# Modulation vectors on VectorE, spread over two layers, and other matmul figures in a planner's cost table

## The chip, the cores and the metric

The kernel runs on one core of a Trainium2 chip, as one launch. The metric is the device time of that launch in microseconds. Every time below is from three timed runs of the kernel before, or from one further execution that was recorded by the hardware profiler.

## What is computed

Two models stand behind each other, on 512 tokens of width 1024 in float32. The first has two hybrid layers: a gated delta rule (GDN, four heads), latent attention (MLA, eight heads) and a linear recurrence (LRU), each behind one input projection, then an output projection that is added to x. The second model has one layer with differential attention, a two-way retention and a mixture of 64 experts. It needs six modulation vectors, which depend on no token:

```python
mod_x = silu(c) @ ada_w + ada_b           # c: (1, 1024), ada_w: (1024, 6144)
mod_c = silu(c_ctx) @ ada_w + ada_b
sh1, sc1, g1, sh2, sc2, g2 = split(mod_x, 6)     # of mod_c the layer uses sh1 and sc1
hx = rmsnorm(x) * (1 + sc1) + sh1                # first use, once both hybrid layers are done
```

So the work on the modulation (called ada in the code) can be done at any time before the second model begins, in the shadow of the two hybrid layers.

## The kernel before

The kernel does not call the engines directly. Every operation is first recorded (class Rec, method add) with its inputs, its outputs and a duration from a table of costs (Rec.cost), in nanoseconds. Then a list scheduler (Rec.plan and Rec.attempt) sets the order of each engine's instructions and of the DMA queue on SyncE: of the operations that are ready by its own clock, the one with the highest priority (the longest remaining path, plus a bias) goes next, if the buffers that it needs are free. The order is then fixed in the program; on the chip each engine runs its own list in that order and waits where an input is late. All instructions are issued from one helper line, so line numbers tell nothing in this profile, and groups are told apart by tile names: raw are seven buffers of 128x1024 for weights that come by DMA, b are 128x512 work buffers, m small ones, ps the eight PSUM banks.

A hybrid layer goes like this. Its input is normalized and transposed (norm_T), and weights of the input projection are loaded in blocks of 512 KB (raw<-in_wi_dram). Each block is split on ScalarE and VectorE into a rounded high part and a low rest (split: an ACTIVATE and a TENSOR_TENSOR for each 128x512), and three fp32r matmuls stand for one product (mm3). TensorE thus waits for VectorE's splits, and VectorE also empties PSUM. In a first stage the chain of GDN is merged with the dense projections; in a second one the eight attention heads are merged with output projections. K.layer merges generators by weights, and a third generator, side, may be merged into both stages: that is ada. The layer ends with x written to DRAM for a later use (xd<-b), by layer 0 and by layer 1 alike.

K2.ada takes the six parts of ada_w in blocks of 128x1024, eight for each part: 48 loads of 512 KB (raw<-in_adaw_dram) into four of the raw buffers (tag ad). Parts 0 and 1 are needed for two vectors, so there are 64 products of a block with a column of numbers: ScalarE scales the block, and GpSimd adds it to the accumulator, but for the first product of each accumulator, which stands alone (64 ScalarE instructions, 56 GpSimd ones). A matmul with a vector of ones then sums over the partitions. K2.ahead wraps that generator: it raises the bias of its operations by 1,000,000, so that whichever is ready goes before anything else on its engine. With the weights SIDE, the generator ends within layer 0. Two lists of windows (WIN, WINA) hold other operations back by their place in the recording.

## Time and profile before

| | us |
|---|---|
| median of three runs | 2389.94 (2387.89 to 2395.32) |
| profiled execution | 2396.73 |
| its span, first to last instruction | 2395.0 |
| TensorE busy | 2187.3 (91%) |
| VectorE busy | 1619.6 (68%) |
| ScalarE busy | 1087.7 (45%) |
| GpSimd busy | 534.6 (22%) |

The profiled execution is 6.79 us above the median, and lies 1.73 us above its own span. Busy time on TensorE is modelled and counts pipelined matmuls whole. In a row of a timeline the first number is the start in us from the span's start, the second the duration; x3 merges three instructions that follow each other; brackets give the idle time before and what ended it. A chain of waits follows the work that ended last back through what released it.

### The profile page before, as it was taken

What the parts mean: (1) busy time and instruction counts of PE and PEld (TensorE: products, weight loads), DVE (VectorE), ACT (ScalarE), POOL (GpSimd) and SP (SyncE); (2) the same over time, 40 slices, a digit from 0 to 9 for tenths busy, and PEclk for the clock granted to TensorE, in tenths of its full rate; (3) what the DMA queues carried; (4) which work ended last, traced back from release to release, by engine and by line L of the source; (5) the groups of instructions that cost most, each with busy time, mean ns of one, the idle gap of its engine ahead of it and who ended that gap; (6) DMA issues with size and microseconds to landing.
All of it is one profiled execution on the core that took longest, in us unless ns stands there. A gap on an engine that the chain in (4) does not pass through costs nothing.

```text
span 2395.0 us, 32613 instructions
## 1 busy us (share of the span) xinstructions
PE 2187.3 (91%) x10382; PEld 1546.5 (65%) x10382; DVE 1619.6 (68%) x3578; ACT 1087.7 (45%) x2272; POOL 534.6 (22%) x393
## 2 busy tenths in 40 slices
PE   6898988999999999999998879879998999999995
PEld 4677866677788877777886657656555555444442
DVE  7995577775695557767733675657676667776775
ACT  5555456453452365445432353335444444544443
POOL 3364334200021010001000132033232233222222
PEclk9998999899999999999998979989999999999998
DMA  5334354223222232314211025349999899999994
GB/s 191 119 102 127 118 172 146 86 84 124 94 78 74 78 116 75 92 63 143 71 54 53 23 66 198 132 116 348 288 341 282 267 294 313 340 334 302 307 311 130
DMA packets 191185, 398.13 MB, mean 166 GB/s; under 512 B 32169, under 2 KB 48297, under 8 KB 191010
## 3 DMA queue, kind: packets, MB, share of 16 engines
q1 hardware_dynamic: 178050, 356.24, 44.1%
q0 software_dynamic: 12960, 39.79, 7.6%
q8 instruction: 82, 1.34, 0.2%
q14 instruction: 93, 0.76, 0.1%
HBM read 358.44 MB, written 41.63 MB: 167 GB/s over the span
## 4 chain that ended last, share of the span: by engine, by line
PE 69%; DVE 13%; DMA 11%; ACT 3%; issue 3%; POOL 1%; SPq 0%; POOLq 0%; DVEq 0%; ACTq 0%
PE ps L411 69%; DVE b L411 10%; DMA raw<-h2d,m 5%; DVE m L411 3%; ACT b L411 3%; DMA accd<-raw,m 1%; DMA raw<-in_adaw_dram 1%; DMA raw<-in_wo_dram 1%; DMA b<-in_ew_dram 1%; POOL raw L411 1%; DMA xdiag<-b 0%; DMA raw<-in_wi_dram 0%; SPq L411 0%; DMA raw<-accd 0%; DMA b<-in_x_dram 0%
## 5 line engine op out<-in xcount | busy, mean ns | idle before, releaser
L411 PE MATMUL ps<-b,b 128*128 128x512 f32 (+9 forms) x8052 | 1870.1, 389 | 83.2 <-DVE b L411 49.6
L411 PEld LDWEIGHTS ps<-b,b 128*128 128x128 f32 (+6 forms) x8052 | 1312.6, 184 | 571.9 <-issue 130.1
L411 ACT ACTIVATE b<-ps 128x512 f32<-128x512 f32 (+16 forms) x661 | 271.1, 431 | 676.6 <-PE ps L411 599.6
L411 DVE TENSOR_TENSOR b<-b,b 128x512 fp32r<-128x512 f32 (+5 forms) x751 | 469.8, 664 | 35.2 <-ACT b L411 18.3
L411 ACT ACTIVATE b<-b 128x512 fp32r<-128x512 f32 (+3 forms) x702 | 393.8, 619 | 121.6 <-DVE b L411 84.5
L411 DVE TENSOR_TENSOR b<-raw,b 128x512 fp32r<-128x512 f32 (+2 forms) x340 | 240.0, 720 | 187.2 <-ACT b L411 173.7
L411 ACT ACTIVATE b<-raw 128x512 fp32r<-128x512 f32 (+3 forms) x348 | 207.2, 611 | 350.3 <-PE ps L411 256.0
L411 POOL DMA_INDIRECT accd<-raw,m x72 | 133.2, 1850 | 367.6 <-DVE raw L411 224.3
L411 PE MATMUL ps<-const,b 128*128 128x128 f32 (+5 forms) x898 | 159.5, 292 | 52.1 <-DVE b L411 39.0
L411 PEld LDWEIGHTS ps<-const,b 128*128 128x128 f32 (+5 forms) x898 | 115.0, 153 | 102.0 <-DVE b L411 49.4
L411 POOL TENSOR_TENSOR raw<-raw,raw 128x1024 f32<-128x1024 f32 x56 | 140.2, 2512 | 159.9 <-ACT raw L411 132.3
L411 PE MATMUL ps<-raw,b 128*96 128x512 f32 (+5 forms) x272 | 151.8, 676 | 5.3 <-ACT raw L411 2.9
L411 POOL DMA_INDIRECT raw<-h2d,m x68 | 100.9, 1483 | 231.0 <-PE ps L411 83.7
L411 DVE SCALAR_TENSOR_TENSOR raw<-ps,m,b 96x512 f32<-96x512 f32 (+5 forms) x136 | 97.5, 740 | 50.9 <-DMA accd<-raw,m 30.1
L411 DVE SCALAR_TENSOR_TENSOR b<-b,ps 128x512 f32<-128x512 f32 (+6 forms) x106 | 54.1, 510 | 102.7 <-ACT b L411 99.2
L411 POOL TENSOR_TENSOR m<-m,mhalf 128x1 f32<-128x1 f32 (+2 forms) x54 | 52.2, 968 | 301.6 <-DVE m L411 301.6
L411 DVE TENSOR_REDUCE m<-ps 128x1 f32<-128x256 f32 (+9 forms) x196 | 75.1, 393 | 60.5 <-PE ps L411 59.0
L411 DVE TENSOR_TENSOR b<-b,ps 128x512 f32<-128x512 f32 (+6 forms) x150 | 82.6, 559 | 49.2 <-PE ps L411 48.5
L411 DVE TENSOR_TENSOR b<-ps,b 128x512 fp32r<-128x512 f32 (+8 forms) x136 | 74.0, 545 | 47.1 <-ACT b L411 38.9
L411 POOL MEMSET b<- 64x512 f32 (+4 forms) x19 | 8.4, 454 | 398.1 <-PE ps L411 326.6
L411 DVE SCALAR_TENSOR_TENSOR b<-ps,cols,b 128x511 f32<-128x511 f32 (+3 forms) x118 | 86.9, 742 | 7.8 <-ACT b L411 6.9
L411 PE MATMUL ps<-const,raw 96*128 96x96 f32 (+5 forms) x544 | 61.0, 249 | 33.4 <-DMA raw<-h2d,m 30.4
(139 smaller groups left out, 1199.0 us busy)
## 6 DMA issues: line engine op xcount, KB each, us to landing
b<-in_ew_dram SPq DMA_DIRECT2D x640, 256.0 KB
raw<-in_wi_dram SPq DMA_DIRECT2D x100, 512.0 KB
raw<-in_ew_dram SPq DMA_DIRECT2D x64, 512.0 KB
raw<-in_adaw_dram SPq DMA_DIRECT2D x48, 512.0 KB
raw<-in_wo_dram SPq DMA_DIRECT2D x40, 512.0 KB
raw<-in_wuq_dram SPq DMA_DIRECT2D x24, 192.0 KB
b<-in_x_dram SPq DMA_DIRECT2D x16, 256.0 KB
zd<-b SPq DMA_DIRECT2D x16, 256.0 KB
```

The costliest lines, as they stand in the source:

```text
L411: getattr(getattr(nc, o.eng), o.fn)(*[real(x) for x in o.a], **{m: real(x) for m, x in o.k.items()})
```

## The change

GpSimd's part in ada goes. Where ScalarE scaled a block and GpSimd added it, VectorE now does both in one instruction (scalar_tensor_tensor, 128x1024, with the column of numbers as its scalar and the accumulator as in place input and output). The first product of each accumulator stays on ScalarE. So 56 ScalarE and 56 GpSimd instructions are replaced by 56 VectorE ones.

The generator is cut into portions of 14 steps: 14 in each of the two stages of layer 0, then in those of layer 1 (there are 54 steps, nine for each part). And each of its operations gets a gate: it cannot be planned before the operation that was recorded 60 earlier has been.

In the table of costs an fp32r matmul with at least 256 columns costs 0.4167 ns a column plus 14 ns, where it was plus 3; a float32 one costs 24 ns more, with a floor of 224 where it was 216. These numbers change no instruction, but the order of all of them.

```diff
--- before.py
+++ after.py
@@ -2,6 +2,7 @@
 import heapq
 import math
 from contextlib import ExitStack
+from itertools import islice
 
 import numpy as np
 
@@ -33,13 +34,15 @@
 XAHEAD = 6
 XBIAS = 6900.0
 NATIVE = 4
-SIDE = ((160, 351), (130, 122))
+SIDE = (11, 12.5)
+SIDEN = 14
 NSLOT = 80
 NADA = 4
 TAGS = {"wl": 5, "wh": 5, "s2": None}
 NRAW = 7
 ADAPS = "tr"
 ADABIAS = 1000000.0
+ADALEAD = 60
 TAIL = 200
 WIDE = (4, 6)
 LAST = 1
@@ -311,8 +314,8 @@
             if dt == BF16:
                 return max(w, 54)
             if dt == F32R:
-                return w + 3 if size(ins[1]) >= 256 else max(4 * w, 108)
-            return max(4 * w, 216)
+                return w + 14 if size(ins[1]) >= 256 else max(4 * w, 108)
+            return max(4 * w + 24, 224)
         if eng == "scalar":
             return 70 + 0.87 * n + (200 if len(outs) > 1 else 50 if len(ins) > 1 else 0)
         if eng == "vector":
@@ -1373,7 +1376,7 @@
         self.pairs, self.mixB = {}, []
         dense = chain(self.lru(l), self.mla_lat(l), self.mz(l))
         parts = [(self.gdn_chain(l), GW[l]), (dense, 100)]
-        run(merge(*parts, *([(side, SIDE[l][0])] if side else [])))
+        run(merge(*parts, *([(islice(side, SIDEN), SIDE[0])] if side else [])))
         self.load_x()
         self.rope_tables(self.A["const"], 256)
         src = lambda nh, k: self.A["wo"][l, nh, k]
@@ -1388,7 +1391,7 @@
                 if h == 3:
                     self.part = list(self.mixB)
 
-        run(merge((heads(), 100), (dense, 60), *([(side, SIDE[l][1])] if side else [])))
+        run(merge((heads(), 100), (dense, 60), *([(islice(side, SIDEN), SIDE[1])] if side else [])))
         run(self.out_proj(src, 4, self.part))
         run(self.out_proj(src, 8, self.mixB[4:8], last=True))
         self.dump_x(f"x{l}")
@@ -1433,12 +1436,14 @@
         g = iter(g)
         while True:
             self.nc.bias += ADABIAS
+            self.nc.gate = max(len(self.nc.ops) - ADALEAD, 0)
             try:
                 w = next(g)
             except StopIteration:
                 return
             finally:
                 self.nc.bias -= ADABIAS
+                self.nc.gate = None
             yield w
 
     def ada(self):
@@ -1461,10 +1466,8 @@
                     f = sc[:, 8 * v + k:8 * v + k + 1]
                     if not k:
                         nc.scalar.activation(acc[v], w, AF.Copy, scale=f)
-                        continue
-                    pr = w if v == nv - 1 else self.t2(tag="ad")
-                    nc.scalar.activation(pr, w, AF.Copy, scale=f)
-                    nc.gpsimd.tensor_tensor(out=acc[v], in0=acc[v], in1=pr, op=OP.add)
+                    else:
+                        nc.vector.scalar_tensor_tensor(acc[v], w, f, acc[v], op0=OP.mult, op1=OP.add)
                 yield 1.0
             if part < 2:
                 for v in range(nv):
```

The order that comes out differs on every engine. GpSimd's list at the start of layer 0 stood like this before: the last of the powers for the first norm (mhalf holds -0.5), four additions into the accumulators raw_147 and raw_148, and four selects that build a mask:

```order
L411 TENSOR_TENSOR m_25_101<-m_23_99,mhalf 128x1
L411 TENSOR_TENSOR raw_147<-raw_147,raw_145 128x1024
L411 TENSOR_TENSOR raw_148<-raw_148,raw_146 128x1024
L411 TENSOR_TENSOR raw_147<-raw_147,raw_146 128x1024
L411 TENSOR_TENSOR raw_148<-raw_148,raw_145 128x1024
L411 AFFINE_SELECT b_447<-b_447 128x128
L411 AFFINE_SELECT b_453<-b_453 128x128
L411 AFFINE_SELECT b_461<-b_461 128x128
L411 AFFINE_SELECT b_467<-b_467 128x128
```

In the kernel after the change that place reads:

```order
L414 TENSOR_TENSOR m_16_92<-m_15_91,mhalf 128x1
L414 AFFINE_SELECT b_369<-b_369 128x128
L414 AFFINE_SELECT b_481<-b_481 128x128
L414 AFFINE_SELECT b_487<-b_487 128x128
L414 AFFINE_SELECT b_492<-b_492 128x128
L414 TENSOR_TENSOR m_13_89<-m_9_85,mhalf 128x8
L414 TENSOR_TENSOR m_15_91<-m_11_87,mhalf 128x8
L414 TENSOR_TENSOR m_20_96<-m_14_90,mhalf 128x8
```

The additions are gone from it (56 in the whole list), and nothing is put in their place.

On VectorE in the second stage of layer 1, where the weights of the keys and values (128x256) and the first ones of the output projection are split, the rows before were these; b<-raw,b is the low part of a split:

```order
L411 TENSOR_TENSOR b_7262<-raw_151,b_7258 128x256
L411 SCALAR_TENSOR_TENSOR b_7268<-b_7230,ps_67 128x512
L411 TENSOR_TENSOR b_7274<-ps_68,b_7264 128x512
L411 SCALAR_TENSOR_TENSOR b_7211<-b_7199,b_7211 128x512
L411 TENSOR_TENSOR b_7286<-ps_65,b_7280 128x512
L411 TENSOR_TENSOR b_7294<-raw_151,b_7290 128x256
L411 TENSOR_REDUCE m_32_108<-ps_72 128x1
L411 TENSOR_TENSOR b_7325<-raw_151,b_7314 128x512
```

After the change VectorE's rows at that place are these, with raw_147 and raw_148 as accumulators and m_30 as the column of numbers:

```order
L414 SCALAR_TENSOR_TENSOR raw_148<-raw_146,m_30_106,raw_148 128x1024
L414 TENSOR_TENSOR b_7089<-raw_149,b_7084 128x384
L414 TENSOR_TENSOR raw_147<-ps_70,raw_147 1x512
L414 TENSOR_TENSOR raw_147<-ps_69,raw_147 1x512
L414 TENSOR_TENSOR b_7116<-raw_149,b_7105 128x256
L414 SCALAR_TENSOR_TENSOR raw_147<-raw_145,m_30_106,raw_147 128x1024
L414 TENSOR_TENSOR b_7140<-raw_149,b_7134 128x256
L414 SCALAR_TENSOR_TENSOR raw_147<-raw_148,m_30_106,raw_147 128x1024
L414 SCALAR_TENSOR_TENSOR raw_147<-raw_146,m_30_106,raw_147 128x1024
L414 TENSOR_TENSOR b_7171<-raw_149,b_7168 128x512
```

Between the splits of such weights there now stand four of the new instructions and two short additions that end a part. 13 of the 21 new instructions of layer 1 stand within 46 rows around this place. The other 35 of the 56 stand in layer 0; eight times in all, a new instruction reads a raw buffer that another of them has read no more than five rows earlier, so that one load has to come between the two.

The DMA queue on SyncE began like this, with the two loads of ada_w, the identity matrix (const) and the first of eight loads of x:

```order
L411 DMA raw_145<-in_adaw_dram 128x1024
L411 DMA raw_146<-in_adaw_dram 128x1024
L411 DMA const_152<-in_const_dram 128x256
L411 DMA b_187<-in_x_dram 128x512
L411 DMA b_190<-in_x_dram 128x512
```

It now begins with the eight loads of x, of which the last two stand here, and what follows them:

```order
L414 DMA b_200<-in_x_dram 128x512
L414 DMA b_202<-in_x_dram 128x512
L414 DMA raw_149<-in_wi_dram 128x1024
L414 DMA const_152<-in_const_dram 128x256
L414 DMA cols<-in_cols_dram 128x2x102
L414 DMA raw_150<-in_wi_dram 128x1024
```

The loads of ada_w have left the head of the queue (the first two stand 23 places further down), and the identity matrix now comes behind x and one weight block.

## Rows read from the trace of the kernel before

**Rows 1.** Busy time by stretch: layer 0, layer 1, and everything after

```profile
core 0: us, PE busy (x) PEld busy (x) DVE busy (x) ACT busy (x) POOL busy (x), PEclk, DMA share, GB/s
8.00:594.00 586.00, 527.99 (x2543) 416.88 (x2544) 422.50 (x860) 301.61 (x558) 186.26 (x111) 0.94 0.39 124
594.00:1107.00 513.00, 501.81 (x2556) 406.26 (x2555) 344.20 (x778) 238.58 (x494) 47.49 (x56) 0.99 0.29 92
1107.00:2395.00 1288.00, 1157.55 (x5285) 723.38 (x5284) 852.30 (x1933) 545.70 (x1220) 298.87 (x217) 0.93 0.67 214
```

**Rows 2.** Timeline: first dense matmuls and writing of x, in both layers

```profile
40.83 22.91 PE L411 MATMUL ps<-b,b 128*128 128x512 f32 x92
...
592.81 4.50 SPq L411 DMA_DIRECT2D xd<-b  x3
...
624.25 15.93 PE L411 MATMUL ps<-b,b 128*128 128x512 f32 x69
...
1105.84 6.04 SPq L411 DMA_DIRECT2D xd<-b  x4
```

**Rows 3.** Chain of waits, shares by releaser, for 8 to 594 and 594 to 1107

```profile
by line: PE ps L411 58.7%; DVE b L411 19.8%; DVE m L411 6.4%; issue 3.9%; ACT b L411 2.8%; DMA raw<-in_adaw_dram 2.8%; DMA raw<-in_wo_dram 1.4%; DMA b<-in_x_dram 0.9%; POOL raw L411 0.9%; DMA raw<-in_wkv_dram 0.7%; DMA xdiag<-b 0.6%; ACT ra
by line: PE ps L411 83.9%; DVE b L411 7.1%; ACT b L411 2.5%; DMA raw<-in_wo_dram 1.6%; issue 1.0%; DMA raw<-in_wuq_dram 0.9%; DMA xdiag<-b 0.8%; DMA raw<-in_wi_dram 0.7%; DMA b<-xdiag 0.6%; ACT L411 0.5%; DVE m L411 0.4%; POOL m L411 0.1%; 
```

**Rows 4.** Instruction groups by shape: the two that the change replaces

```profile
L411 POOL TENSOR_TENSOR raw<-raw,raw 128x1024 f32<-128x1024 f32 x56 | 140.2, 2512 | 159.9 <-ACT raw L411 132.3 <-DVE b L411 17.3 <-PE ps L411 6.9
L411 ACT ACTIVATE raw<-raw,m 128x1024 f32<-128x1024 f32 x64 | 73.1, 1144 | 17.1 <-DMA raw<-in_adaw_dram 12.1 <-PE ps L411 4.6 <-DMA modr<-raw 0.3
```

**Rows 5.** Timeline of layer 0: VectorE instructions beside GpSimd additions, and without

```profile
15.80 0.15 DVE L411 TENSOR_TENSOR m<-m,m 128x4 f32<-128x4 f32 x1
...
19.01 4.66 POOL L411 TENSOR_TENSOR raw<-raw,raw 128x1024 f32<-128x1024 f32 x2 [4.21 <-ACT raw L411]
...
21.39 2.39 DVE L411 TENSOR_TENSOR m<-m 128x4 f32<-128x4 f32 x2
...
356.25 0.69 DVE L411 SCALAR_TENSOR_TENSOR b<-b,b 128x512 f32<-128x512 f32 x1
...
357.76 2.63 POOL L411 TENSOR_TENSOR raw<-raw,raw 128x1024 f32<-128x1024 f32 x1 [4.91 <-ACT raw L411]
...
358.23 2.70 DVE L411 SCALAR_TENSOR_TENSOR b<-b,b 128x512 f32<-128x512 f32 x1
```

**Rows 6.** Timeline and groups: VectorE's scalar_tensor_tensor of 1024 and of 512

```profile
408.57 1.20 DVE L411 SCALAR_TENSOR_TENSOR raw<-raw,raw 1x1024 f32<-1x1024 f32 x1
...
L411 DVE SCALAR_TENSOR_TENSOR b<-b,ps 128x512 f32<-128x512 f32 x38 | 25.9, 682 | 15.6 <-ACT b L411 14.8 <-DVE b L411 0.5
...
L411 DVE SCALAR_TENSOR_TENSOR b<-b,m,b 128x512 f32<-128x512 f32 x32 | 23.3, 750 | 0.2
```

**Rows 7.** Pieces of the chain of waits: loads of ada_w; and a total of waits

```profile
55.21 4.51 DMA raw<-in_adaw_dram
...
278.25 6.18 DMA raw<-in_adaw_dram
...
300.61 5.50 DMA raw<-in_adaw_dram
...
ACT raw L411 <- DMA raw<-in_adaw_dram: 12.1, 8, 3.1
```

**Rows 8.** Timeline at the start: queue, first use of x

```profile
0.77 0.88 SPq L411 DMA_DIRECT2D raw<-in_adaw_dram  x2
...
7.48 0.63 ACT L411 ACTIVATE b<-b 128x512 f32<-128x512 f32 x1 [5.42 <-DMA b<-in_x_dram]
```

**Rows 9.** Timeline: a run of matmuls that waits for nothing

```profile
406.14 10.89 PE L411 MATMUL ps<-b,b 128*128 128x512 f32 x47
```

**Rows 10.** The page: TensorE and DMA in 40 slices of 59.9 us, in tenths

```profile
PE   6898988999999999999998879879998999999995
DMA  5334354223222232314211025349999899999994
```

## The prediction

> **What bounds the kernel now.** I read the busy time by stretch first, because the kernel holds a comparison within itself: layer 0 and layer 1 do the same work, and ada stands in layer 0 alone. The stretch from 8 us (x arrives) to 594 is layer 0, the one to 1107 is layer 1 [rows 1]. TensorE runs 2543 and 2556 instructions in them, so its work is equal. Yet layer 0 lasts 586 us and layer 1 513. In layer 1 TensorE idles 513 - 501.8 = 11 us at a granted clock of 0.99; in layer 0 58 us, at 0.94. Layer 1 is bound by TensorE; layer 0 loses time to something else.
>
> To leave the start out of it, I took the same two events from the timeline in both layers [rows 2]: the first dense run of matmuls and the first write of x. They lie 592.81 - 40.83 = 552.0 us apart in layer 0, and 1105.84 - 624.25 = 481.6 in layer 1. The excess is 70.4 us, with no start-up in it.
>
> The chain of waits then says on whom TensorE waits [rows 3]. In layer 1 it holds the chain for 83.9%, VectorE for 7.5%. In layer 0 it is 58.7% against 26.2% for VectorE, and the loads of ada_w have 2.8%. So VectorE is late in layer 0, though its busy share there (422.5 of 586 us, 72%) is hardly above layer 1's (344.2 of 513, 67%).
>
> The timeline shows why [rows 5]. A VectorE instruction on 128x4 takes 0.15 us, but two of them beside GpSimd's additions took 2.39 together. A scalar_tensor_tensor of 128x512 takes 0.69; the one that began 0.47 us after an addition of 2.63 took 2.70, and ended 0.54 us after that addition. VectorE thus stands still until GpSimd's addition is over, and the stall is booked as its own busy time.
>
> **The change part by part.** *GpSimd's additions go.* There are 56, of 2.51 us [rows 4], all in layer 0. What they cost VectorE is bounded by the stretches [rows 1]: 422.5 - 344.2 = 78.3 us more busy in layer 0, of which its 82 additional instructions, at the 0.15 to 0.2 us of small ones, explain some 16. That leaves 62 us of stalls; the excess between the marks is 70.4. I count 65 us as recovered, between the two. It could be as little as 50, as the GDN chain has another merge weight in the two layers (300, 584) and part of the excess may be that, and as much as 75, if stalls before the first dense run go too. GpSimd's own 140 us, and 56 ScalarE products of 1.14 us (64 us), free engines that the chain hardly names; I give them nothing of their own, as the 65 us already hold whatever they cost.
>
> The Trainium skill, "SBUF — State Buffer", section "Who interferes with whom", has this as a rule: VectorE and GpSimd share a port pair, and an instruction of VectorE with two SBUF inputs and one of GpSimd that reads SBUF exclude each other for a whole instruction. The stall of 2.70 us agrees. The same rule speaks against the change too, as the new instruction has two SBUF inputs: GpSimd is busy 47.5 of 513 us in layer 1 [rows 1], so some 5 of 56 would meet one of its instructions, for about 0.85 us each (47.5 / 56). By it the sum would lose 1 us (5 x 0.85 x 0.25); I leave that out.
>
> *VectorE takes 56 instructions of 128x1024.* The trace has one scalar_tensor_tensor of 1024 elements in a row, at 1.20 us, on one partition and without a column as scalar; at 512 elements the column costs 0.750 - 0.682 = 0.07 [rows 6]. So 1.27 us each, 71.1 in all: 35 in layer 0 and 21 in layer 1. They cannot gain time; at worst all 71.1 lie on the path. How much does? In layer 1 the chain gives VectorE 7.5% of 513 = 38 us, out of 344 busy: 0.11 of each busy microsecond. In layer 0 it is 26.2% of 586 = 154 out of 422: 0.36. I take 0.25, since the new instructions come first whenever ready and stand close together, but with four PSUM banks and TensorE's queue of matmuls to hide behind: 71.1 x 0.25 = 18 us (8 to 26 by the two shares).
>
> *VectorE now waits for loads of ada_w in its own order.* Behind a late one stand the splits of the next weight block, and TensorE waits for those. Before, ScalarE waited 12.1 us in 8 cases [rows 7]. The chain shows loads of 4.51, 5.50 and 6.18 us, 5.4 in the mean; the planner allows 3.5 (by the code 60 ns to issue, 512 KB at 360 bytes a nanosecond, 2000 ns to land). Where one load has to come between two nearby instructions on the same buffer, which the order shows eight times, about 1.9 us is short: 15 us, of which the layer 0 share (0.36) is 5. None at the least; 42 loads x (6.18 - 3.5) = 113 at worst. On SyncE's queue the next weight loads stand behind such a load; they were behind ada_w loads before as well.
>
> *The start.* Two 512 KB loads no longer stand ahead of x, whose first use came at 7.48 us, after 5.42 of waiting [rows 8]. The queue spends 0.88 us on issuing them, and their transfer delays x as well: 2 us. Nothing, if the identity matrix, now behind x and a weight block, arrives later than the norm does; at most the 4.5 of a whole load.
>
> *The planner's matmul figures.* A run of 47 matmuls of 512 columns took 10.89 us, 0.232 each [rows 9]; the old table says 0.216, the new one 0.227. So the planner's clock comes nearer to the chip's. After 1107 TensorE idles 1288 - 1157.6 = 130 us [rows 1], and that is what a new order there can win or lose. No row prices an order, and I take zero; a third of that idle, 39 us, either way bounds it.
>
> **Sum.** -65 - 2 + 18 + 5 = -44 us, against the profiled execution's 2396.73: 2352.7. It stood 6.8 us above the median of the runs, so I forecast 2346.
>
> **The rivals.** *A better order afterwards (2307).* With truer figures the idle after 1107 shrinks by the 39 us: -83. For it: TensorE is busy only 7 or 8 tenths in five of the six slices from 1257 to 1617 us. Against: from there on its matmuls run beside loads that keep the DMA engines at 0.8 or more in every slice but the last [rows 10], and no order shortens those.
>
> *A worse order afterwards (2385).* The same 39 us lost: -5. The windows that hold operations back count recorded operations, of which there are now 56 fewer, and were not moved with them.
>
> *VectorE time for VectorE time (2386).* If each of its microseconds is worth the same, wherever it stands, the change gives back 78.3 and takes 71.1: -7 - 2 + 5 = -4. For it: its total busy time would hardly move. Against: the stalls strike small instructions in the middle of a chain, while the new ones wait for nothing but a load, and layer 1 has slack.
>
> *Loads late for VectorE (2421, slower than before).* Place: the new instructions in both attention stages. Price: not 8 but all 42 are short by 1.9 us, 80 in all, with nothing hidden: -67 + 18 + 80 = +31. It decides from 49 / 42 = 1.2 us per load on the path. For it: most loads go through one buffer. Against: the planner spaced them so that they should have landed, and VectorE has free time between.
>
> That the work is not spread as meant is true in part (13 of 21 instructions of layer 1 in 46 rows, 17 us there); if that stretch stopped TensorE wholly, the sum would be 12 us worse, within the forecast's own range.
>
> **How the numbers follow.** Forecast 0.66, with its own range from 2321 (75 recovered, 8 for the new instructions, no waits) to 2379 (50 recovered, 26 and 15). Better order 0.12, worse order 0.07, exchange 0.09, late loads 0.06. The range for 8 in 10 goes from 2303, within the better order, to 2384. About 0.3%, 7 us, can be told from no change. Faster: 0.66 + 0.12 and about 0.04 of the two cases near 2385. Those give most of the 0.11 for the same; slower is 0.07, the late loads and a rest of a worse order.
>
> **What would show it.** After the change layer 0, from its first dense run to its first write of x, should take 495 to 515 us instead of 552, at a clock near 0.99, and layer 1 485 to 495. VectorE's share of the chain in layer 0 should fall from 26% to 10 to 15%. No small VectorE instruction should take 2.4 us there any more. The new instructions should take 1.2 to 1.3 us; VectorE's busy time should stay within 15 us of 1620, ScalarE's fall by 64 and GpSimd's by 140. VectorE's waits for loads of ada_w should total 10 to 25 us. The stretch behind layer 1 should stay within 15 us of 1288. The forecast is wrong if layer 0 keeps its excess though the stalls are gone, if layer 1 grows by more than 20 us, or if the stretch behind moves by more than 25.

## The result, and the profile after

The changed kernel takes 2425.25 us (median of 4 runs, 2423.0 to 2429.05), the kernel before 2390.71 beside it. The ratio is 1.0143, with an interval of 1.0126 to 1.016: slower by 34.5 us, where 44 us less was forecast. The profiled execution has a span of 2421.3 us.

The windows of the kernel after, with the columns of [rows 1]: layer 0, layer 1, all that follows, and of that the expert phase alone (from GpSimd's first gather to the first reading back of the sums, accd).

```profile
8.00:548.00 540.00, 508.64 (x2522) 406.38 (x2523) 383.99 (x886) 241.42 (x493) 47.73 (x54) 0.96 0.36 114
548.00:1088.00 540.00, 519.43 (x2571) 411.54 (x2570) 371.23 (x804) 238.88 (x495) 49.52 (x56) 0.97 0.34 109
1088.00:2421.00 1333.00, 1180.94 (x5292) 731.56 (x5290) 853.74 (x1934) 546.16 (x1223) 332.13 (x217) 0.91 0.66 207
1558.00:2403.00 845.00, 764.71 (x3161) 399.99 (x3159) 548.94 (x1189) 361.23 (x782) 276.73 (x148) 0.93 0.88 274
```

The expert phase of the kernel before, in the same view:

```profile
1575.00:2378.00 803.00, 744.54 (x3152) 389.90 (x3151) 551.62 (x1189) 361.84 (x782) 243.55 (x148) 0.95 0.91 288
```

Beside [rows 1], layer 0 became 46 us shorter, layer 1 27 us longer, and everything behind 45 us longer, 42 of that in the experts. TensorE does the same matmuls there, yet is busy 20 us more at a lower clock, and idles 80 us instead of 58. GpSimd is busy 33 us more.

The chain of waits of the kernel after, in layer 0 and in layer 1, against [rows 3]:

```profile
by line: PE ps L414 77.7%; DVE b L414 7.5%; ACT b L414 4.2%; DMA raw<-in_wo_dram 2.7%; issue 1.7%; DVE raw L414 1.5%; ACT L414 1.2%; DMA raw<-in_wi_dram 1.1%; DVE m L414 0.7%; DMA xdiag<-b 0.6%; DMA b<-xdiag 0.5%; DMA raw<-in_wkv_dram 0.5%;
by line: PE ps L414 79.6%; DVE b L414 7.6%; ACT b L414 3.2%; DMA raw<-in_wo_dram 2.5%; issue 1.6%; POOL b L414 1.2%; DVE raw L414 0.7%; DMA b<-mdiag 0.7%; DMA raw<-in_wi_dram 0.6%; DMA xdiag<-b 0.5%; DMA b<-xdiag 0.5%; ACT L414 0.5%; DMA md
```

In layer 0 VectorE's share fell from 26.2% to 9.7%, and ada_w is gone from it. The groups that answer to [rows 4] and [rows 6], and a total of waits that answers to [rows 7]:

```profile
L414 DVE SCALAR_TENSOR_TENSOR raw<-raw,m,raw 128x1024 f32<-128x1024 f32 x56 | 72.4, 1314 | 5.0 <-DMA raw<-in_adaw_dram 2.8 <-ACT raw L414 2.2
```
```profile
DVE raw L414 <- DMA raw<-in_adaw_dram: 2.8, 2, 2.2
```

So in layer 0 the modulation did what was forecast. The larger part of the loss lies in the experts (42 us, against 27 in layer 1). There the chain reads as follows, before (first fence) and after (second); raw<-h2d,m is GpSimd's gather of token rows for the next expert block:

```profile
by line: PE ps L411 69.8%; DMA raw<-h2d,m 16.1%; DMA accd<-raw,m 3.7%; DMA b<-in_ew_dram 2.4%; issue 2.3%; ACT b L411 1.9%; DVE b L411 1.3%; SPq L411 0.6%; DVE m L411 0.5%; POOL raw L411 0.4%; DVE raw L411 0.4%; ACT raw L411 0.2%; POOL accd
```
```profile
by line: PE ps L414 57.6%; DMA raw<-h2d,m 24.1%; DMA accd<-raw,m 7.5%; DMA b<-in_ew_dram 2.5%; issue 2.1%; DVE b L414 1.6%; DVE raw L414 1.3%; POOL accd L414 1.0%; DVE m L414 0.7%; POOL raw L414 0.6%; SPq L414 0.4%; ACT b L414 0.3%; ACT raw
```

TensorE's own waits for that gather (us in total, times, longest), before and after:

```profile
PE ps L411 <- DMA raw<-h2d,m: 30.4, 15, 4.7
```
```profile
PE ps L414 <- DMA raw<-h2d,m: 61.9, 25, 5.0
```

They doubled, to 31 us more. And the 68 gathers themselves take longer on GpSimd (groups, before and after; after the bar busy time and mean ns):

```profile
L411 POOL DMA_INDIRECT raw<-h2d,m x68 | 100.9, 1483 | 231.0 <-PE ps L411 83.7 <-issue 59.2 <-DVE m L411 51.8
```
```profile
L414 POOL DMA_INDIRECT raw<-h2d,m x68 | 135.8, 1997 | 176.0 <-DVE m L414 73.4 <-issue 46.4 <-PE ps L414 40.4
```

The timeline shows one of them. First the kernel before, in an expert block of 80 rows:

```profile
1996.59 2.62 POOL L411 DMA_INDIRECT accd<-raw,m  x1 [4.57 <-DVE b L411]
...
2000.26 0.14 DVE L411 TENSOR_SCALAR m<-m 80x1 int32<-80x1 f32 x1
...
2001.19 1.00 POOL L411 DMA_INDIRECT raw<-h2d,m  x1 [1.98 <-PE ps L411]
...
2001.66 1.90 DVE L411 TENSOR_TENSOR b<-b,b 128x512 fp32r<-128x512 f32 x3 [0.19 <-issue]
```

Then the kernel after, in a block of the same size:

```profile
2000.25 1.70 POOL L414 DMA_INDIRECT accd<-raw,m  x1 [9.05 <-DVE m L414]
...
2000.96 0.14 DVE L414 TENSOR_SCALAR m<-m 80x1 int32<-80x1 f32 x1
...
2002.25 4.09 POOL L414 DMA_INDIRECT raw<-h2d,m  x1 [0.30 <-issue]
...
2002.38 3.09 DVE L414 TENSOR_TENSOR b<-b,b 128x512 fp32r<-128x512 f32 x5
...
2012.09 1.26 PE L414 MATMUL ps<-const,raw 80*128 80x80 f32 x8 [3.10 <-DMA raw<-h2d,m]
```

In both, VectorE makes the row numbers (int32), and GpSimd issues the gather with them. Before, VectorE's run of splits began 0.47 us after the gather, which took 1.00. After, GpSimd was first at the issue of a scatter (accd<-raw,m), so the gather began later, 0.13 us ahead of a run of five splits, with VectorE busy up to it. It took 4.09 us and ended 0.87 us after that run. TensorE's transposes then waited 3.10 us. Of the 24 gathers above 1.5 us in the kernel after, 23 ended 0.83 to 0.92 us after the last split of a run. Before, 16 were above 1.5 us.

A run of splits does not hold every gather beside it. In the kernel before, in a block of 32 rows, this one began 1.09 us into a run and took 1.02 us; what makes the difference was not found:

```profile
2315.30 3.09 DVE L411 TENSOR_TENSOR b<-b,b 128x512 fp32r<-128x512 f32 x5
...
2316.39 1.02 POOL L411 DMA_INDIRECT raw<-h2d,m  x1 [0.30 <-issue]
```

### The profile page after: what moved, and what is told of

Same layout as the page of the kernel before. It is cut to its first block, busy times and chain, and to the rows that moved or that the text cites. A ratio compares the mean times of both kernels' runs of the same rounds, so it can differ in the third digit from the quotient of the medians.

```text
span 2421.3 us, 32518 instructions
## 1 busy us (share of the span) xinstructions
PE 2209.0 (91%) x10382; PEld 1549.5 (64%) x10382; DVE 1610.1 (66%) x3634; ACT 1030.0 (43%) x2216; POOL 431.9 (18%) x337
## 3 DMA queue, kind: packets, MB, share of 16 engines
q8 instruction: 82, 1.34, 0.2%
## 4 chain that ended last, share of the span: by engine, by line
PE 69%; DMA 15%; DVE 9%; ACT 3%; issue 2%; POOL 1%; SPq 0%; POOLq 0%; DVEq 0%; ACTq 0%
PE ps L414 69%; DMA raw<-h2d,m 8%; DVE b L414 7%; DMA accd<-raw,m 3%; ACT b L414 2%; DVE m L414 1%; DMA raw<-in_wo_dram 1%; DVE raw L414 1%; DMA b<-in_ew_dram 1%; DMA raw<-in_wi_dram 0%; ACT L414 0%; POOL accd L414 0%; POOL b L414 0%; DMA raw<-accd 0%; POOL raw L414 0%
## 5 line engine op out<-in xcount | busy, mean ns | idle before, releaser
L414 PE MATMUL ps<-b,b 128*128 128x512 f32 (+10 forms) x8052 | 1875.6, 390 | 77.1 <-DVE b L414 37.4
L414 DVE TENSOR_TENSOR b<-b,b 128x512 fp32r<-128x512 f32 (+5 forms) x751 | 459.7, 646 | 28.9 <-ACT b L414 13.3
L414 ACT ACTIVATE b<-b 128x512 fp32r<-128x512 f32 (+3 forms) x702 | 395.0, 621 | 133.0 <-DVE b L414 100.9
L414 DVE TENSOR_TENSOR b<-raw,b 128x512 fp32r<-128x512 f32 (+2 forms) x340 | 226.6, 678 | 188.3 <-ACT b L414 177.5
L414 POOL DMA_INDIRECT raw<-h2d,m x68 | 135.8, 1997 | 176.0 <-DVE m L414 73.4
L414 PE MATMUL ps<-raw,b 128*96 128x512 f32 (+5 forms) x272 | 161.2, 708 | 2.7 <-ACT raw L414 2.4
L414 PE MATMUL ps<-const,raw 48*128 48x48 f32 (+5 forms) x544 | 68.6, 264 | 63.1 <-DMA raw<-h2d,m 61.9
L414 PEld LDWEIGHTS ps<-const,raw 48*128 48x128 f32 (+5 forms) x544 | 54.6, 157 | 93.4 <-DMA raw<-h2d,m 73.7
L414 DVE COPY b<-ps 128x128 f32<-128x128 f32 (+2 forms) x134 | 50.3, 381 | 61.1 <-PE ps L414 50.8
```

What stands on the lines that cost most here:

```text
L414: getattr(getattr(nc, o.eng), o.fn)(*[real(x) for x in o.a], **{m: real(x) for m, x in o.k.items()})
```

## The experiments

The stages are cut at four events of the trace: the first write of x by layer 0 (counted from 8 us), the first by layer 1, the first gather, and the first reading back of accd. "Gathers" is their busy time on GpSimd, "waits" what TensorE waited for them. All times are in us; each run had the kernel before (2390 to 2392) beside it. In the three runs marked with a star the sums of the modulation are left out, so other rows go to other experts, which have 17 blocks more to do; of these only the layers are read.

A stage time comes from one profiled execution, which can lie some 7 us from the median. The layers of after, e11 and e14 hold the same instructions in the same order, and their times agree within 1.7 us (layer 0) and 2.2 us (layer 1); differences of that size tell nothing. The expectations of e1, e2 and e4 count the expert stage from some 30 us later: their 773 and 815 are the 803 and 846 of the table.

| run | median | ratio, interval | layer 0 | layer 1 | block behind | experts | gathers | waits |
|---|---|---|---|---|---|---|---|---|
| before | 2390.7 | 1 | 584.8 | 513.0 | 468.6 | 803.3 | 100.9 | 30.4 |
| after | 2425.3 | 1.0126 to 1.016 | 539.7 | 540.3 | 469.6 | 845.6 | 135.8 | 61.9 |
| e1_figures | 2476.7 | 1.0331 to 1.0398 | 591.1 | 531.0 | 472.2 | 856.1 | 139.7 | 70.6 |
| e2_ada | 2358.8 | 0.9832 to 0.9913 | 529.0 | 524.1 | 473.9 | 801.0 | 104.5 | 32.3 |
| e3_vector | 2383.0 | 0.995 to 0.9994 | 558.7 | 513.7 | 469.8 | 814.1 | 109.9 | 34.0 |
| e4_figures_early | 2375.2 | 0.9906 to 0.996 | 539.7 | 541.5 | 467.9 | 805.5 | 98.5 | 24.8 |
| e5_f32r | 2457.0 | 1.0231 to 1.0291 | 602.3 | 526.7 | 470.9 | 832.6 | 126.7 | 53.2 |
| e6_f32 | 2451.8 | 1.0191 to 1.0265 | 584.4 | 524.4 | 468.9 | 850.1 | 134.2 | 55.3 |
| e7_new_steps | 2366.5 | 0.9847 to 0.9912 | 542.0 | 541.1 | 467.3 | 790.2 | 83.1 | 16.3 |
| e8_old_steps | 2355.7 | 0.981 to 0.9869 | 530.0 | 526.5 | 474.2 | 797.4 | 94.0 | 18.9 |
| e9_no_adds * | | | 516.5 | 508.8 | | | | |
| e10_no_sums * | | | 532.8 | 537.9 | | | | |
| e11_one_input | 2375.4 | 0.9918 to 0.9964 | 540.8 | 538.1 | 471.3 | 802.5 | 90.8 | 41.5 |
| e12_both | 2362.6 | 0.9857 to 0.9914 | 537.4 | 524.9 | 473.4 | 804.0 | 86.2 | 27.8 |
| e13_before_one_input | 2434.3 | 1.0147 to 1.0198 | 583.9 | 512.7 | 472.2 | 841.7 | 71.0 | 33.5 |
| e14_one_input_long | 2393.0 | 0.9998 to 1.0032 | 539.1 | 539.1 | 472.4 | 817.1 | 70.9 | 32.9 |
| e15_no_loads * | | | 535.5 | 535.2 | | | | |

**The two halves apart.** e1_figures is the kernel before with only the new figures; e2_ada is the changed kernel with the old ones.

```diff
-                return w + 3 if size(ins[1]) >= 256 else max(4 * w, 108)
-            return max(4 * w, 216)
+                return w + 14 if size(ins[1]) >= 256 else max(4 * w, 108)
+            return max(4 * w + 24, 224)
```

> The kernel before with the new matmul figures alone (ada stays on ScalarE and GpSimd, all in layer 0). Theory A: the new figures reorder the expert stage, which after the change took 815 us (1588 to 2403) where it took 773 before (1605 to 2378), and the modulation has no part in that. Then the expert stage is 815 here too, the layers stay near their 586 and 513 us, and the time is about 2390 + 42 = 2432 (2420 to 2440). Rival B: the expert stage is longer because of the modulation (other recorded places, another state at the start of the stage); then the time is within 8 us of 2391.

> The kernel after with the old matmul figures: VectorE accumulates, spread over both layers, with the gate. Theory A: expert stage back at 773 us; layer 0 at about 540 instead of 586, layer 1 at about 540 instead of 513, so 2391 - 46 + 27 = 2372 (2362 to 2380). Rival B: expert stage 815, time 2415 or more. If layer 1's 27 us come from the figures and not from the instructions that moved into it, the time is 2345 to 2360.

The figures alone cost 85 us, 53 of it in the experts; 42 in all were expected. The layers grew too, by 6 and 18. Without them the change gains 33 us by the medians; by the stages it is 56 in layer 0, less 11 in layer 1 and 5 behind it, where the two profiled executions lie 41 us apart. With layer 1 at 524.1, some 16 of its 27 us come from the figures. Put on top of the change they cost 2425.3 - 2358.8 = 66.5, by stages 11 + 16 - 4 + 45 = 68. So the cause of the loss is the figures, through the order that they give.

**VectorE instead of GpSimd, unspread.** e3_vector is the kernel before with all 56 instructions on VectorE in layer 0, without portions or gate.

```diff
-                    nc.gpsimd.tensor_tensor(out=acc[v], in0=acc[v], in1=pr, op=OP.add)
+                        nc.vector.scalar_tensor_tensor(acc[v], w, f, acc[v], op0=OP.mult, op1=OP.add)
```

> The kernel before with the products accumulated on VectorE alone: old weights and so all in layer 0, no gate, old figures. If the stalls behind GpSimd's additions were what cost layer 0 its excess, and the 56 instructions cost a quarter of their 71 us, layer 0 is 586 - 65 + 18 = 539, layer 1 stays at 513, and the time is 2345 (2330 to 2360). If VectorE's time is exchanged one for one, 2384 (2378 to 2392).

The 2345 us that were expected were missed. The total of 2383.0 is the one of the even exchange (2384), but the stages are not: by that rival layer 0 gains 78.3 - 71.1 = 7 us, and it gained 26. The experts lost 11 without a figure of theirs having been touched; VectorE's order there is another one, so it hangs on what the stages before leave behind.

**The figures by place and by kind.** e4_figures_early is the changed kernel with the old figures in the experts' phase alone; e5_f32r and e6_f32 are the kernel before with one of the two lines of the diff above each.

```diff
+        Rec.fig = (3, 0) if self.phase == 3 else (14, 24)
```

> The kernel after with the old figures for what is recorded in the last stage (expert stage, routing and shared expert), the new ones ahead of it. Theory A (the loss is made by the figures within the expert stage itself): expert stage near 773, time 2425 - 42 = 2383 (2373 to 2392). Rival: the loss comes from how the stages ahead leave the planner's state (their order moves the expert stage as well): expert stage 795 or more, time above 2405.

> The kernel before with the fp32r figure alone (plus 14 ns instead of 3). Theory C (coincidence): the expert stage is slow where VectorE's sum that makes the index of a coming block stands within four rows of the last product of a finished block, so that GpSimd's scatter of the one runs just ahead of the gather of the other. That is so for 29 of 65 blocks in the kernel before (expert stage, first gather to the reading back of the sum, 803 us) and for 44 with both figures (846 and 856), some 3 us for each. Here it is 37: 803 + 8 x 3 = 827 us; the layers as with both figures (591 and 531); time about 2391 + 24 + 22 = 2437 (2420 to 2450). Rival F (each figure adds its share): half of the 85 us for each, 2433 and the same in layers and experts.

> The kernel before with the float32 figure alone (plus 24 ns, floor of 224). Theory C: 35 of 65, so the expert stage takes 803 + 6 x 3 = 821 us; the layers, whose matmuls of 512 columns are all fp32r, stay within 5 us of 585 and 513; time about 2410 (2398 to 2420). Rival F: 2433.

In e4 the experts fall by 40 us, and the layers stay as in the changed kernel: the loss in the experts is made by the figures of their own phase. Each figure alone costs more than 60 us and makes the gathers slow (126.7 and 134.2), so it is not one of them that is at fault. Both times were forecast too low, by 20 and 42 us. Theory C, which counts blocks where a scatter stands just ahead of a gather, came near in the experts of e5 (827 for 832.6), but not in those of e6 (821 for 850.1).

**Two numbers that are measured in the planner's clock.** STEP, the spacing of the expert blocks, and XBIAS, the advance of the exchange operations, are in its nanoseconds. e7_new_steps raises both in the changed kernel, e8_old_steps in e2_ada.

```diff
-STEP = 4800.0
+STEP = 5400.0
-XBIAS = 6900.0
+XBIAS = 8000.0
```

> The kernel after, new figures kept, with two other numbers of the expert stage's priorities: 5400 instead of 4800 for the step from expert to expert, 8000 instead of 6900 for the lead of an index and its gather. Theory C: only 22 of 65 now coincide, so the expert stage takes 780 to 803 us instead of 846, the layers stay at 540 and 540, and the time is 2425 - 43 to 65 = 2360 to 2382. Rival F (the new figures are bad for the stage whatever the priorities): expert stage 840 or more, time within 10 us of 2425.

> VectorE's accumulation spread over both layers with the old figures (as in e2_ada, 2359 us and an expert stage of 801), but with 5400 and 8000 for the same two priorities. Theory C: 41 of 65 coincide, expert stage 830 to 845, time 2359 + 30 to 44 = 2389 to 2403. Rival F: old figures, so expert stage near 801 and time within 10 us of 2359.

With the same figures as the changed kernel, e7 has the shortest expert phase of all, 790.2, and one gather above 2.5 us (23 in the changed kernel, 8 before). The truer figures are therefore not bad for the experts in themselves; beside the old STEP and XBIAS they put the gathers in a bad place. In the layers they still cost 12 and 15 us (e7 less e8). Theory C failed in e8: 830 to 845 us were forecast for the experts, and they took 797.4. Its count alone does not price an order. In e7 a block of 80 rows reads:

```profile
1994.93 0.99 POOL L414 DMA_INDIRECT raw<-h2d,m  x1 [2.03 <-DMA b<-in_ew_dram]
...
1995.38 1.29 DVE L414 TENSOR_TENSOR b<-b,b 128x512 fp32r<-128x512 f32 x2 [0.19 <-DMA b<-in_ew_dram]
```

The run of splits begins 0.45 us after the gather, much as before the change (0.47).

**The price of the modulation.** e9_no_adds leaves the GpSimd additions out of the kernel before, e10_no_sums the new VectorE instructions out of the changed kernel, e15_no_loads the 42 loads as well; in all three the planned order stands. Their edit marks an operation when it is recorded, and skips it when the program is written out:

```diff
+                    nc.ops[-1].mark = "skip"
...
+            if o.mark == "skip":
+                continue
```

> The kernel before, in its own order, without the 56 GpSimd additions of the modulation vectors; what is left out is the sum over the 64 rows, while the loads and ScalarE's products stay. Theory (VectorE stood still behind these additions, 65 us worth): layer 0 falls from 584.8 to about 520 us, layer 1 stays at 513 and the experts at 803, since nothing of their order moves; 2391 - 65 = 2326. Rival (the excess of layer 0 is mostly the other merge weight and the order of its chain): layer 0 falls by 30 us or less, 2360 or more. Against the run with the VectorE accumulation alone (layer 0 558.7), the difference in layer 0 is then the price of 56 VectorE instructions standing in that layer: about 38 us by the theory.

> The changed kernel, in its own order, without the 56 VectorE instructions of the modulation vectors; what is left out is the sum over the 64 rows, while the loads stay. Theory (a quarter of their busy time lies on the path, and the rest of what the layers gained or lost is order): layer 0 falls from 539.7 by 11 us to about 528, layer 1 from 540.3 by 7 to about 533, the experts stay at 846; 2425 - 18 = 2407. Rival (layer 1 grew by 27 us because of these instructions): layer 1 falls to about 515 and the total to about 2385.

> The changed kernel, in its own order, without the 56 VectorE instructions of the modulation vectors and also without the 42 loads of ada_w that only they read; only the layers can be read from it, since with these sums left out other rows go to the experts. Theory (layer 1 grew by 27 us through the order of its other instructions, by the figures and by where the planner puts them around the new ones): layer 1 stays at 530 to 538, as without the 56 instructions alone (537.9). Rival (the loads of ada_w, which now run beside layer 1's weights, delay those): layer 1 falls to about 520, and layer 0 from 532.8 to about 520.

For e9 the windows give these rows for layer 0 and layer 1:

```profile
8.00:524.50 516.50, 500.47 (x2538) 400.51 (x2539) 352.06 (x859) 298.38 (x554) 45.94 (x55) 0.99 0.44 140
524.50:1033.00 508.50, 496.53 (x2554) 401.29 (x2554) 343.59 (x776) 238.25 (x492) 47.66 (x56) 1.00 0.30 93
```

Without the additions layer 0 falls by 68.3 us, VectorE's busy time by 70 and the clock is back at 0.99: the stalls were worth what was forecast (a part of it may be loads that came earlier: ScalarE's waits for ada_w fell from 12.1 to 7.0 us). The total times expected for e9 and e10 were missed, as I had not thought of the routing. The 56 new instructions cost 6.9 us in layer 0 and 2.4 in layer 1, where 11 and 7 were expected; the 42 loads cost nothing that can be told (layer 0 took 2.7 us longer without them, layer 1 2.7 less). So of layer 1's 27 us at most 5 come from what was put into it; the rest is the order.

Pieces of that rest are seen. After a wait of TensorE for a round trip through DRAM in layer 1 (chain of waits of the kernel after)

```profile
692.35 2.95 DMA xdiag<-b
...
695.36 2.82 DMA b<-xdiag
...
698.23 1.97 PE ps L414 x8
```

the clock stood at its lower level for a window of 9 us (windows):

```profile
692.00:701.00 9.00, 6.50 (x31) 5.49 (x29) 3.56 (x11) 1.21 (x3) 2.78 (x2) 0.84 0.59 156
701.00:710.00 9.00, 9.00 (x44) 8.70 (x43) 2.03 (x4) 0.77 (x2) 0.00 (x0) 0.50 0.02 6
710.00:719.00 9.00, 9.00 (x63) 8.20 (x63) 6.72 (x12) 1.40 (x3) 0.00 (x0) 0.90 0.08 23
```

The kernel before has the same wait (1.69 us) and one window at a lower clock behind it, so this place explains only a few us:

```profile
747.00:756.00 9.00, 8.86 (x50) 8.56 (x50) 1.75 (x3) 1.15 (x3) 0.00 (x0) 0.62 0.19 57
```

A later stretch has no counterpart there: before the change the clock is 1.00 in every window of layer 1 behind this one. In the kernel after, TensorE has six gaps between 860 and 881 us, 6.8 us together, and the clock falls:

```profile
863.00:872.00 9.00, 5.39 (x14) 2.15 (x14) 7.44 (x10) 8.14 (x19) 2.38 (x2) 0.82 0.57 204
872.00:881.00 9.00, 7.96 (x23) 6.33 (x24) 9.00 (x12) 6.73 (x12) 3.18 (x2) 0.61 0.33 91
```

e10, without the new instructions, has such a stretch too (0.56 and 0.87), which again speaks for the order. In all of layer 1 TensorE had 8 gaps above 0.35 us before, 9 us together, and 17 after, 19 us together. Which moved operation opens each gap was not tried.

**What makes the gathers slow.** e11_one_input is the changed kernel in its own order, in which the low part of the experts' splits is made from one SBUF tensor instead of two.

```diff
+                for s in (slice(0, 511), slice(511, 512)):
+                    nc.vector.tensor_scalar(out[:, s], src[:, s], hi[:, 0:1], None, op0=OP.subtract)
```

> The changed kernel, in its own order, where the low part of the expert weights' splits is made with one tensor input instead of two: a column of the high part is subtracted as a scalar, on 511 columns and on one more. Left out is the true low part. Theory (GpSimd's gathers take long because they are issued while VectorE runs instructions with two tensors from SBUF): the gathers, 2.0 us in the mean and 135.8 in sum, fall to about 1.1 to 1.3 us each and 75 to 90 in sum, TensorE's waits for them from 61.9 us to 25 or less, and the experts from 846 to about 800 or below, by the same slope as in the runs so far (1.2 us per us of gather time); 2425 - 45 = 2380. Rival (the gathers are slow because the scatter just ahead of them still runs, or they are merely put too late in the order): their durations stay near 2.0 us and the experts near 846; 2425. The 520 additional VectorE instructions of one column, at about 0.1 us, cost some 50 us of VectorE time in the experts, which may take back part of the gain.

The experts fall by 43 us to 802.5, with every instruction in its place, and the gathers from 135.8 to 90.8; the waits fall to 41.5 only, where 25 or less was expected. But VectorE was also busy 39 us less in the experts (510.0 for 548.9), which could have given that by itself. So e14_one_input_long has three instructions on the last column instead of one, and e13_before_one_input the same edit in the kernel before.

```diff
-                for s in (slice(0, 511), slice(511, 512)):
+                for s in (slice(0, 511), slice(511, 512), slice(511, 512), slice(511, 512)):
```

> The kernel before, in its own order, with the low part of the expert weights' splits made with one tensor input (a column of the high part subtracted as a scalar, on 511 columns, and then three instructions on one column, so that VectorE is not sooner done than with one instruction of 0.68 us). Left out is the true low part. Theory (instructions with two tensors from SBUF make the gathers beside them slow, and the change only put more gathers beside them): the gathers, 100.9 us in sum, fall to 85 to 92, as with the same edit in the changed kernel, and the experts from 803 by some 5 to 15 us, since fewer slow gathers are waited for here (8 above 2.5 us, against 23 after the change); 2391 - 10 = 2381. Rival (what the edit gained in the changed kernel, 43 us in the experts, came from a VectorE that was sooner done): the experts stay at 803 or grow, since VectorE now is not.

> As the changed kernel with one tensor input in the expert weights' splits, but with three instructions on one column instead of one, so that a split takes VectorE as long as the 0.68 us of the instruction with two inputs, or longer. Left out is the true low part. Theory (two inputs make the gathers slow): gathers of about 91 us in sum, the experts at 800 to 812; 2375 to 2387. Rival (VectorE was sooner done, 510 instead of 549 us of busy time in the experts, and that gave the 43 us): the experts go back to 835 or more, with gathers still near 91; 2410 or more.

In e14 the window of the experts, the group of the gathers and a place of the timeline read:

```profile
1558.00:2380.00 822.00, 749.17 (x3163) 392.96 (x3163) 708.03 (x2710) 362.37 (x786) 190.32 (x148) 0.95 0.92 283
```
```profile
L419 POOL DMA_INDIRECT raw<-h2d,m x68 | 70.9, 1042 | 175.6 <-DVE m L419 79.3 <-PE ps L419 34.3 <-issue 27.7
```
```profile
1996.36 1.09 DVE L414 TENSOR_SCALAR b<-b,b 128x511 fp32r<-128x511 f32 x4
...
1996.99 0.99 POOL L419 DMA_INDIRECT raw<-h2d,m  x1 [0.56 <-issue]
...
1997.89 5.16 DVE L414 TENSOR_SCALAR b<-b,b 128x511 fp32r<-128x511 f32 x20
```

The edit overshot: VectorE is busy 708 us, 159 more than in the changed kernel, and the total of 2393.0 lies between the two forecasts. Even so the experts are 28 us shorter than there, and the gathers take 1.04 us in the mean and 1.41 at most, where 23 took more than 2.5. A VectorE that is sooner done is therefore not what the gain needs. Nor is the scatter ahead to blame by itself: in e14, 28 gathers follow a scatter within 0.4 us, and none of them took over 1.22 us; in the changed kernel 19 of 32 such took more than 1.5. In the kernel before, the same burden cost 38 us (e13, where 10 us less was expected): the price of VectorE's time I had left out, and few slow gathers were there to win back. e13 alone therefore tells nothing apart; the two together do. With all gathers short, TensorE waits for them equally in both orders (33.5 and 32.9 us), and the new order (817.1) even beats the old one (841.7).

The Trainium skill, "SBUF — State Buffer", section "Who interferes with whom", says that a VectorE instruction with two SBUF inputs and a GpSimd instruction that reads SBUF exclude each other. The rows of the changed kernel agree, if issuing a gather counts as reading its row numbers: one took 4.09 us beside a run of such instructions. But e11 shows that two tensors as inputs are not needed. There the splits have one, and eight gathers still took 2.51 to 4.14 us, one of them (2.67 us, from 1844.53) with nothing but such splits beside it. The gather of the block of 80 rows shown above reads in e11:

```profile
2001.39 2.81 POOL L419 DMA_INDIRECT raw<-h2d,m  x1 [0.30 <-PE ps L419]
...
2001.56 2.66 DVE L414 TENSOR_SCALAR b<-b,b 128x511 fp32r<-128x511 f32 x10
```

So the theory of e11, e13 and e14, that the two inputs make the gathers slow, is not shown. With one column instruction in each split (e11) the mean is 1.34 us, with three (e14) 1.04. In e14's trace some 0.035 us lie between instructions on the same column, where otherwise the records of VectorE's instructions overlap. That an unbroken run holds a gather, and such a pause lets it through, is the nearest reading; no run tests it by itself.

**The halves put together.** e12_both takes the old figures up to the experts, the new ones with 5400 and 8000 there.

```diff
+        Rec.fig = (14, 24) if self.phase == 3 else (3, 0)
```

> A version put together from the runs so far: the modulation vectors on VectorE as in the changed kernel, the old matmul figures in the attention layers and in the block behind them, and in the expert phase the new figures with a window of 5400 instead of 4800 and a bias of 8000 instead of 6900 for the exchange. If the stages add up, layer 0 takes 529 us and layer 1 524 as with the old figures, the block behind them 474, and the experts 790 as in the run with the new figures and those two numbers: 2425 - 11 - 16 + 4 - 56 = 2346, where the best so far is 2355.7. Rival (an order's cost in the experts hangs on what the stage before it leaves over, so that stages don't add up): the experts take 800 to 815, 2356 to 2371.

Its rival came true: the gathers are short (86.2), but the waits are 27.8 us instead of e7's 16.3, and the experts take 804.0. The stages don't add up. Layer 0 took 537.4 where 529 was expected, which stays unexplained. The fastest version is e8_old_steps at 2355.7, 1.6% below the kernel before and, with e2_ada at 2358.8, one of two that can't be told apart.

## Why the prediction was wrong

The sign was wrong, and one step made it so: "No row prices an order, and I take zero; a third of that idle, 39 us, either way bounds it." The planner's figures cost 66 us beside the rest of the change and 85 alone. Behind layer 1 they cost 40 (56 alone), against the bound of 39, and in the layers 27, which the term left out. The idle time that is there does not bound a loss: layer 1 had 11 us of it and grew by 27, of which at most 5 come from what was put into it. A worse order makes new idle time: in the experts TensorE idles 80 us instead of 58, and its work takes 20 us more at a granted clock of 0.93 instead of 0.95. What the runs showed in place of the zero is a wait: the new order put more of GpSimd's gathers where VectorE's splits held them up (135.8 us instead of 100.9), and TensorE's waits for them went from 30.4 to 61.9 us.

The rival that I gave 7%, the worse order, had the right place, behind layer 1, at a price of 39; the 27 us in the layers no case of mine held, and its reason (windows that count recorded operations) was not the one found. The case of the late loads came nearest in number (2421), by luck: VectorE waited 2.8 us for them.

The other terms, as the runs priced them:

| term | forecast | measured |
|---|---|---|
| stalls behind the additions | -65 | -68 in layer 0 (e9) |
| start: first use of x | -2 | at 3.54 us instead of 7.48, so some -4 |
| 56 VectorE instructions | +18 | +9 (e10), of 72.4 busy; unspread +42 (e3 less e9, with its other order) |
| loads of ada_w | +5 | waits of 2.8; nothing in e15 |
| order, apart from the figures | 0 | e2's -33 less the four above: some +30 |
| the figures | 0 | +66 (after less e2) |

That e2's 33 us lie near the forecast of 44 is in part luck: the new instructions and the loads were priced 14 us too high, and some 30 us of order were left out.

*Stalls.* Right in cause and size. In the kernel after, one VectorE instruction in layer 0 still took over 1.4 us (2.32, one of the new ones), where it was 39 before; the small ones on 128x4 take 0.15.

*New instructions.* 1.31 us each, forecast 1.27. On the path lay 9 of 72 us when they are spread; it was 42 when all 56 stood in layer 0, but that run has another order as well, so how much of it is the place stays open. The 0.25 that I took lay between. The rival of an even exchange (VectorE time for VectorE time) is thereby out for the changed kernel, and so are the late loads.

*Marks.* The first dense run of layer 0 now begins at 24.54 us, not at 40.83 as in [rows 2], so 16 of the 45 us that the stage gained lie ahead of the first mark, where my sum had 2. Between the marks it is 547.74 - 24.54 = 523 us, outside the 495 to 515 of the forecast, at a clock of 0.96 and not 0.99. The waits for ada_w (2.8 us) lie below the 10 to 25 that were named. ScalarE fell by 58 (forecast 64), GpSimd by 103 instead of 140, as its gathers grew by 35. Two conditions of failure were met as written: layer 1 grew by more than 20, and the stretch behind it moved by more than 25.

The rows that could have warned: in the experts' stretch the kernel before already waited 30.4 us for gathers, with 16 of them above 1.5 us. I read the stretch behind layer 1 as a sum of idle time, and did not ask which wait ended last in it.

## What to carry to other kernels

When a change touches a planner's costs, constants beside them that are in the same unit (spacings, advances) belong to them: set them together, or price the order as an unknown that can lose more than the idle time that is there (at least 22 us against 11 in layer 1). Try the parts of a change one at a time; here one gained 33 us and hid in a sum that lost 34. Keep transfers that GpSimd issues away from long unbroken runs of VectorE instructions on SBUF tensors, and look in the trace for issues of unequal length with the same shape.

## What the runs showed of the hardware

In the rows above the issue of a gather of 80 rows took from 0.99 to 4.09 us. In the changed kernel 23 of the 24 gathers above 1.5 us ended 0.83 to 0.92 us after VectorE's run of splits, not after one of them; so five splits of 0.68 us held a gather for all five. Runs with one tensor input did so too (eight gathers of 2.51 to 4.14 us in e11), and not every gather beside a run is held (1.02 us beside five splits in the kernel before). And GpSimd's work can be the sufferer: in the layers its additions held up VectorE, in the experts VectorE's splits held up GpSimd.
